# Identity products between two scans, and a blocked triangular solve loaded and stored in parts, in a hybrid DeltaNet and windowed attention layer

## The chip, the cores and the metric

The kernel runs on one core of a Trainium2 chip. The metric is device time in microseconds (us) of one execution of the whole layer. The core's engines are PE (TensorE, matrix products), DVE (VectorE), ACT (ScalarE), POOL (GpSimd) and SP (SyncE, which here issues all DMAs). Each takes its own queue of instructions in order and waits on semaphores of the others.

## The reference

One layer of a bidirectional encoder on x of 2048 x 1024: RMSNorm, one input projection, two groups of heads side by side, an output projection and the residual. Cut to what matters here:

```python
h = rms_norm(x, norm_w)
dn_q, dn_k, dn_v, dn_z, dn_beta, dn_decay, sw_q, sw_k, sw_v, sw_z = split(h @ w_in)
dn = gated_deltanet_bidir(...)           # 4 heads of 128, forward and backward
sw = windowed_gqa_with_sinks(...)        # 8 query heads of 64, |i-j| <= 128
dn = rms_norm(dn, dn_out_norm_w) * silu(dn_z)
sw = sw * silu(sw_z)
x = x + concat([dn, sw]) @ w_out

# gated DeltaNet, one head, one direction, chunk by chunk:
m = tril(k_beta @ k.T, -1) * decay                   # inside a chunk
t_inv = inverse(eye + m)                             # unit lower triangular
u = t_inv @ (v * beta); w = t_inv @ (k_beta * exp(g))
a_intra = incl_tril(q @ k.T) * decay
def step(state, ...):                                # over the chunks, in order
    v_new = u - w @ state
    o = (q * exp(g)) @ state + a_intra @ v_new
    state = state * exp(g_last) + k_dec.T @ v_new
```

So each of the 4 heads needs, for both directions, the inverse of one triangular matrix per chunk, and then a recurrence over the chunks that can't be done in parallel.

## The kernel before, in words

A first phase computes the norm, the projection (products of 512 columns in three parts of a high and a low half), the attention, and the convolutions and gates of the DeltaNet; q, k, v and the gates go to DRAM. What follows is the DeltaNet, with 16 chunks of 128 rows, head by head (h = 0 to 3), in three functions and a fourth that closes a head:

- `pre_front(h)` goes over four groups of four chunks, in the order 1, 2, 0, 3 (`FRONT`). A group loads kq, vt and the decay rows (dc, exponentials on ACT at L669 for all heads but the first), transposes k and q on PE (tr, L641; ks and jk are what ACT makes of them), forms the products gh (L661), scales them on DVE into `ma` (L670, eight operations a group), and stores the rows of ma in DRAM (`m_d`, L675). Then come the transposes of v (trv, L678) and vs (ACT, L682).
- `pre_back(h)` inverts. It loads the 32 x 32 diagonal blocks of all 128 strips (16 chunks x 4 x 2 directions, one strip to a partition) from m_d into `L0` and `L` (two DMAs, L697 and L698), reorders half of them, and runs a forward substitution of 31 steps on DVE, each a product tm (L705) and a subtraction X (L709). This is called the solve. The inverses X go to DRAM (`x_d`, L710) and come back in another layout, per step hi = 0 to 3 a block `xc` for each direction (L718): group hi forward, group 3 - hi backward. DVE transposes it (xt, L719), POOL spreads it into iv (L724 to L728), and five passes of four products on PE (pi, L733) with copies on ACT between them (b and the copies at L742 to L757) build the inverse of the whole 128 x 128 chunk.
- `scan(h)` is the recurrence: 16 steps, each for both directions, forward from chunk 0 and backward from chunk 15. A step loads kqc (L771), and does the products pk, py and po on PE (L773 to L800), r and the state S on DVE, yk and y on ACT, and the sums oacc.
- `post` normalises the output of finished groups (jko, oacc, the transposes tro on PE, zt on DVE) and stores them in `mix_dn` (L843).

The scan of head h needs the inverse for its first chunks at once: forward group 0 and backward group 3, which is hi = 0. Products of the attention half of the output projection (`out_sw`: pcs at L558 to L560, the sums xrs at L561, stored as part) stand in the program between pre_front(0) and pre_back(0). The DeltaNet half of the output projection comes last.

```python
    H = pre_front(0)
    ...                                   # out_sw
    pre_back(0, H)
    for h in range(3):
        scan(h, H)
        H = pre_front(h + 1)
        pre_back(h + 1, H)
    ...
    scan(3, H)
```

This is not the order in which the engines run. A planner (`set_order`) takes all instructions with their dependences and a table of costs, schedules them as a list in several rounds, and writes each engine's queue in the order that it found. So the front and the solve of head h + 1 run beside the scan of head h, and an edit anywhere moves instructions on all five engines.

Buffers are tiles of pools with a number of copies; a tile of the same tag waits for the readers of the copy that it takes over. The PSUM tile `pk` has one copy.

Of the kernel before, what the change touches and what calls it, by code (L numbers as in the profile page):

```python
# [7 lines left out]
F32 = mybir.dt.float32  # L8
# [7 lines left out]
P = 128  # L16
# [3 lines left out]
NCH = 16  # L20
# [496 lines left out]
def phase_b(ctx, tc, t, ident, consts, hp, mix_dn, mix_sw, kq_d, v_d, zdn_d, zsw_d, dp, out):  # L517
    nc = tc.nc
    V, A, G, T = nc.vector, nc.scalar, nc.gpsimd, nc.tensor
    dma = nc.sync.dma_start  # L520

    def pool(name, bufs=1, stack=ctx, **kw):
        return stack.enter_context(tc.tile_pool(name=name, bufs=bufs, reuse_waits="tile", **kw))
# [58 lines left out]
    qp = pool("qp", stack=pre_stack)  # L582
    ps_s = pool("ps_s", space=PSUM)
# [12 lines left out]
    def ma_tile(h, p):  # L596
        tag = f"ma{FREED[p] if h > 1 else p}"
        return hd[h % 2].tile([P, 4, 4, P], F32, tag=tag, name=f"ma{h}_{p}", bufs=1)

    def kv_tile(kind, h, n, name):  # L600
        p, slot = ((0, n), (1, n), (2, n) if n < 2 else (0, n - 2), (0, 2 + n) if n < 2 else (1, n - 2))[h]
        return (hd[p] if p < 2 else qp).tile([P, 4, P], F32, tag=f"{kind}{slot}", name=name, bufs=1)

    def pre_front(h):
        H = {}
        ssk = hp.tile([P, NCH], F32, tag="ssk", name=f"ssk{h}", bufs=1)
        nk = hp.tile([P, NCH], F32, tag="nk", name=f"nk{h}", bufs=1)
        bp = hp.tile([P, 2, NCH], F32, tag="bp", name=f"bp{h}")
        ssq = H["ssq"] = hp.tile([P, NCH], F32, tag="ssq", name=f"ssq{h}", bufs=3)
        ck = H["ck"] = hp.tile([P, 2, NCH], F32, tag="ck", name=f"ck{h}", bufs=3)  # L610
        ks = H["ks"] = {}
        vs = H["vs"] = {}
        mp = {}
        ma = H["ma"] = {}
        m_d = dp.tile([2, NCH, 4 * (32 * P + 32)], F32, tag="m_d", name=f"m_d{h}", bufs=2)
        x_d = dp.tile([2, NCH, P, 32], F32, tag="x_d", name=f"x_d{h}", bufs=2)
        for n, c4 in enumerate(FRONT):
            s4 = slice(4 * c4, 4 * c4 + 4)
            cs = slice(c4 * 512, (c4 + 1) * 512)
            kq = q1.tile([P, 2, 512], F32, tag="kq", name=f"kq{h}_{c4}", bufs=2)  # L620
            dma(kq, kq_d[h][:, :, cs])
            vt = q1.tile([P, 512], F32, tag="vt", name=f"vt{h}_{c4}", bufs=2)
            dma(vt, v_d[h][:, cs])
            gms = []
            for d in range(2):
                gm = q1.tile([P, 4, P], F32, tag="gm", name=f"dc{h}_{c4}_{d}", bufs=4)
                if h < NDEC:
                    dma(gm.rearrange("p c i -> p (c i)"), dec_d[h, d][c4])
                else:
                    src = gr_d[d].rearrange("(c h) i -> c h i", h=4)[s4, h]  # L630
                    dma(gm, src.partition_broadcast(P))
                    G.tensor_tensor(gm, gm, dmask[:, d : d + 1].to_broadcast([P, 4, P]), ALU.add)
                gms.append(gm)
                p = 3 - c4 if d else c4
                if p not in mp:
                    mp[p] = ma_tile(h, p)
                ma[d, c4] = mp[p][:, :, 1 - d :: 2]
            for j, ss in ((0, ssk), (1, ssq)):
                tr = ps_t.tile([P, 4, P], F32, tag="tr", name=f"tr{h}_{c4}_{j}")
                for c in range(4):  # L640
                    T.transpose(tr[:, c], kq[:, j, c * P : (c + 1) * P], ident)  # L641
                if j == 0:
                    ks[c4] = kv_tile("ks", h, n, f"ks{h}_{c4}")
                    A.activation(ks[c4], tr, AF.Copy)
                for c in range(4):
                    cc = 4 * c4 + c
                    src = ks[c4] if j == 0 else tr
                    jk = q1.tile([P, P], F32, tag="jk", name=f"jk{h}_{c4}_{j}_{c}", bufs=3)
                    A.activation(jk, src[:, c], AF.Square, accum_out=ss[:, cc : cc + 1])
            V.tensor_scalar(ssk[:, s4], ssk[:, s4], EPS, None, ALU.add)  # L650
            G.tensor_tensor(nk[:, s4], ssk[:, s4], pw[:, 0, :4], ALU.pow)
            V.reciprocal(ssk[:, s4], ssk[:, s4])
            V.tensor_tensor(
                bp[:, :, s4], beta[:, s4, h :: 4].rearrange("p c d -> p d c"),
                ssk[:, s4].unsqueeze(1).to_broadcast([P, 2, 4]), ALU.mult,
            )
            for c2 in range(2):
                gh = ps_g.tile([P, 2, 2, P], F32, tag="gh", name=f"gh{h}_{c4}_{c2}")
                for k in range(2):
                    c = 2 * c2 + k  # L660
                    T.matmul(  # L661
                        gh[:, k], kq[:, 0, c * P : (c + 1) * P], kq[:, :, c * P : (c + 1) * P], start=True, stop=True
                    )
                for k in range(2):
                    c = 2 * c2 + k
                    cc = 4 * c4 + c
                    for d in range(2):
                        if h >= NDEC:
                            A.activation(gms[d][:, c], gms[d][:, c], AF.Exp, bias=ngc[:, d, cc, h : h + 1])  # L669
                        V.scalar_tensor_tensor(  # L670
                            ma[d, c4][:, c], gh[:, k], bp[:, d, cc : cc + 1],
                            gms[d][:, c : c + 1].to_broadcast([P, 2, P]), ALU.mult, ALU.mult,
                        )
            for d in range(2):
                dma(m_d[d, s4, : P * P].rearrange("u (i j) -> i u j", j=P), ma[d, c4][:, :, 0])  # L675
            tr = ps_t.tile([P, 4, P], F32, tag="tr", name=f"trv{h}_{c4}")
            for c in range(4):
                T.transpose(tr[:, c], vt[:, c * P : (c + 1) * P], ident)  # L678
            vs[c4] = kv_tile("vs", h, n, f"vs{h}_{c4}")
            for c in range(4):  # L680
                cc = 4 * c4 + c
                A.activation(vs[c4][:, c], tr[:, c], AF.Copy, scale=nk[:, cc : cc + 1])  # L682
        for d in range(2):
            V.tensor_tensor(ck[:, d], bp[:, d], ekd[:, d, :, h], ALU.mult)

        H["solve"] = m_d, x_d, mp
        return H

    def pre_back(h, H):
        ma = H["ma"]  # L690
        m_d, x_d, mp = H["solve"]
        L0 = qp.tile([64, 32, 32], F32, tag="L0", name=f"L0{h}")
        L = qp.tile([P, 32, 32], F32, tag="L", name=f"L{h}")
        X = qp.tile([P, 32, 32], F32, tag="X", name=f"X{h}")
        lv = [m_d[d].rearrange("u (p y) -> (u p) y", p=4)[:, : 32 * P] for d in range(2)]
        lv = [a.rearrange("q (r x) -> q r x", x=P)[:, :, :32] for a in lv]
        dma(L0, lv[0])  # L697
        dma(L[64:128], lv[1])  # L698
        dma(X, t["eye32"].partition_broadcast(P))
        V.tensor_copy(L[0:64], L0.rearrange("p r c -> p c r"))  # L700
        for c in range(31):
            n = 31 - c
            tm = qp.tile([P, 256], F32, tag="tm", name=f"tm{h}_{c}")
            tv = tm[:, : n * (c + 1)].rearrange("p (r k) -> p r k", k=c + 1)
            XE.tensor_tensor(  # L705
                tv, L[:, c + 1 :, c : c + 1].to_broadcast([P, n, c + 1]),
                X[:, c : c + 1, 0 : c + 1].to_broadcast([P, n, c + 1]), ALU.mult,
            )
            XE.tensor_tensor(X[:, c + 1 :, 0 : c + 1], X[:, c + 1 :, 0 : c + 1], tv, ALU.subtract)  # L709
        dma(x_d.rearrange("d u (p r) c -> (d u p) (r c)", p=4), X.rearrange("p r c -> p (r c)"))  # L710
        for hi in range(4):
            e1, p2, e2, e3 = (z[hi % len(z)] for z in zts)
            m = mp[hi]
# [1 line left out]
            for d, c4 in ((0, hi), (1, 3 - hi)):  # L715
                xc = qp.tile([P, 4, 32], F32, tag="xc", name=f"xc{h}_{d}_{c4}", bufs=4)
                xt = qp.tile([P, 4, 32], F32, tag="xt", name=f"xt{h}_{d}_{c4}", bufs=4)
                dma(xc, x_d[d, 4 * c4 : 4 * c4 + 4].rearrange("u i c -> i u c"))  # L718
                V.transpose(xt.rearrange("p u c -> p (u c)"), xc.rearrange("p u c -> p (u c)"))  # L719
                x0[d], x1[d] = (xc, xt) if d == 0 else (xt, xc)  # L720
            g = qp.tile([P, 4, P], F32, tag="g", name=f"g{h}_{hi}", bufs=2)
# [111 lines left out]
    def post_rows(h, oa, so, c4):  # L833
# [8 lines left out]
        V.scalar_tensor_tensor(zt, tr.rearrange("p c i -> p (c i)"), dnw, zt, ALU.mult, ALU.mult)  # L842
        dma(mix_dn[h, :, c4 * 512 : (c4 + 1) * 512], zt)  # L843

    H = pre_front(0)
    with tc.using_default_side("right"):
        with ExitStack() as sw:
# [4 lines left out]
            )  # L852
        hd[1] = pool("hd1")
    pre_back(0, H)
    for h in range(3):
        scan(h, H)
        H = pre_front(h + 1)
        pre_back(h + 1, H)
    pre_stack.close()
    op = pool("op", 4)  # L860
    ps_c = pool("ps_c", 4, space=PSUM)
# [362 lines left out]
```

## Time and profile before

| | |
|---|---|
| median of three runs | 1340.53 us (1336.61 to 1341.32) |
| the profiled execution | 1339.74 us, span 1338.0 us |
| mean granted TensorE clock | 0.979 |
| busy: PE, DVE, ACT, POOL | 1258.0, 885.6, 711.3, 484.4 us |
| DMA | 150 GB/s in the mean |

The profile is of one execution. Its views are: the page (busy time, the span in 40 slices with the granted clock of PE in tenths, the costliest groups); busy times of the engines in chosen stretches of time, with the granted clock (1.00 is full speed); the timeline of one engine, where a row gives start, length, line, operation, output and inputs, and in brackets the idle time before it with what ended it; the chain of waits, which follows the end of a stretch back through what released each step; and the time from issue to landing of the DMAs. PE products of fp32 show as two records each.

### The profile page before, as it was taken

The numbers are of one execution on the slowest core, as the hardware profiler recorded it, in microseconds if no ns is written. First come the engines' busy times: TensorE is split into PE (matmuls) and PEld (weight loads), VectorE is DVE, ScalarE is ACT, GpSimd is POOL, SyncE is SP. The second block draws the span as 40 slices with busy tenths as digits, with TensorE's granted clock in tenths as the row PEclk, the third lists the DMA queues.
The fourth block names the chain that finished last, engine by engine and source line by source line (L and its number), as shares of the span: only waits on it lengthen the run. The fifth ranks groups of instructions, "written<-read, shape, count | busy, mean of one in ns | idle before, by whom it ended". The sixth has DMA issues, their size and how long they took to land.

```text
span 1338.0 us, 22553 instructions
## 1 busy us (share of the span) xinstructions
PE 1258.0 (94%) x7162; PEld 1072.9 (80%) x7162; DVE 885.6 (66%) x2250; ACT 711.3 (53%) x2105; POOL 484.4 (36%) x868
## 2 busy tenths in 40 slices
PE   5999999999999999999999899998979879898998
PEld 4998878788998888888888687778868769788776
DVE  4423387773632399999987899666885877846433
ACT  5422264332433467666667877229868766466310
POOL 1223032100021235755786755228238155170000
PEclk8999999999999999999999999999979989989999
DMA  7442345244443533222334757968567274333776
GB/s 235 135 140 78 104 161 171 73 135 135 148 121 114 163 102 109 72 93 83 96 120 130 249 185 226 291 209 217 144 184 207 84 212 104 94 104 106 233 241 209
DMA packets 219686, 201.16 MB, mean 150 GB/s; under 512 B 48304, under 2 KB 170800, under 8 KB 219568
## 3 DMA queue, kind: packets, MB, share of 16 engines
q1 hardware_dynamic: 219568, 199.73, 48.8%
q8 instruction: 57, 0.93, 0.3%
q14 instruction: 61, 0.50, 0.1%
HBM read 134.59 MB, written 65.08 MB: 149 GB/s over the span
## 4 chain that ended last, share of the span: by engine, by line
PE 72%; DVE 9%; DMA 5%; ACT 5%; POOL 5%; issue 3%; SPq 0%; DVEq 0%; POOLq 0%; ACTq 0%
PE pf_c L186 6%; PE pf_c L187 6%; PE pf_c L188 5%; PE pf_z L186 4%; PE pf_z L187 4%; PE pf_z L188 4%; PE pi L733 4%; PE pt L360 2%; PE pq_q L197 2%; PE pq_q L199 2%; PE pq_q L198 2%; PE pcd L559 2%; PE pcd L560 2%; PE pcd L558 2%; PE pcs L558 2%
## 5 line engine op out<-in xcount | busy, mean ns | idle before, releaser
L237 DVE SCALAR_TENSOR_TENSOR acc<-pf_c,cw,acc 128x512 f32<-128x512 f32 (+1 forms) x192 | 140.0, 745 | 22.7 <-ACT acc L233 20.9
L186 PE MATMUL pf_c<-xhi,wh_c 128*128 128x512 f32 x384 | 149.3, 401 | 1.9 <-DVE acc L237 1.1
L187 PE MATMUL pf_c<-xlo,wh_c 128*128 128x512 f32 x384 | 150.4, 401 | 0.0
L188 PE MATMUL pf_c<-xhi,wl_c 128*128 128x512 f32 x384 | 148.4, 400 | 0.0
L186 PE MATMUL pf_z<-xhi,wh_z 128*128 128x512 f32 x256 | 91.6, 400 | 0.1
L355 POOL TENSOR_SCALAR pr<-pr,st 128x384 f32<-128x384 f32 (+1 forms) x128 | 83.5, 670 | 22.5 <-DVE st L353 19.0
L187 PE MATMUL pf_z<-xlo,wh_z 128*128 128x512 f32 x256 | 91.0, 397 | 0.0
L346 ACT ACTIVATE pr<-pr,st 128x384 f32<-128x384 f32 (+1 forms) x128 | 76.2, 598 | 27.3 <-DVE st L345 26.7
L188 PE MATMUL pf_z<-xhi,wl_z 128*128 128x512 f32 x256 | 90.3, 396 | 0.0
L186 PEld LDWEIGHTS pf_c<-xhi,wh_c 128*128 128x128 f32 x384 | 72.3, 189 | 17.5 <-DVE acc L237 1.9
L188 PEld LDWEIGHTS pf_c<-xhi,wl_c 128*128 128x128 f32 x384 | 72.0, 188 | 14.6
L187 PEld LDWEIGHTS pf_c<-xlo,wh_c 128*128 128x128 f32 x384 | 72.3, 188 | 13.9
L341 DVE CUSTOM_DVE_ANT_0 pr<-s,mask,sink 128x384 f32<-128x384 f32 (+1 forms) x128 | 72.6, 594 | 6.0 <-PE pt L360 2.5
L360 PE MATMUL pt<-ident,pr 128*128 128x128 f32 x368 | 72.8, 276 | 3.3 <-ACT q L323 1.4
L364 ACT ACTIVATE ph<-pt 128x512 fp32r<-128x512 f32 x92 | 53.4, 594 | 40.2 <-PE pt L360 37.3
L365 DVE TENSOR_TENSOR pl<-pt,ph 128x512 fp32r<-128x512 f32 x92 | 62.5, 684 | 9.1 <-ACT ph L364 7.9
L670 DVE SCALAR_TENSOR_TENSOR ma<-gh,bp,dc 128x256 f32<-128x256 f32 x128 | 56.1, 476 | 17.7 <-PE gh L661 10.0
L787 ACT ACTIVATE yk<-py,ck 128x128 f32<-128x128 f32 x120 | 44.0, 367 | 40.4 <-PE py L782 39.1
L360 PEld LDWEIGHTS pt<-ident,pr 128*128 128x128 f32 x368 | 48.6, 141 | 19.2 <-POOL pr L355 4.8
L178 DVE TENSOR_TENSOR wl_c<-ws_c,wh_c 128x512 fp32r<-128x512 f32 x48 | 36.6, 765 | 37.0 <-ACT wh_c L177 24.7
L197 PE MATMUL pq_q<-wh_q,xhi 128*128 128x256 f32 x256 | 58.5, 284 | 0.8 <-ACT sgq L256 0.8
L561 DVE TENSOR_TENSOR xrd<-xrd,pcd 128x512 f32<-128x512 f32 x32 | 20.9, 684 | 55.5 <-PE pcd L560 55.5
(250 smaller groups left out, 3769.9 us busy)
## 6 DMA issues: line engine op xcount, KB each, us to landing
kqc<-kq_d SPq DMA_DIRECT2D x120, 128.0 KB, 2.5
ws_c<-wt SPq DMA_DIRECT2D x48, 256.0 KB, 3.5
xr<-x SPq DMA_DIRECT2D x16, 512.0 KB, 6.0
ws_z<-wt SPq DMA_DIRECT2D x32, 256.0 KB, 3.4
kq<-kq_d SPq DMA_DIRECT2D x16, 512.0 KB, 4.9
xrs<-x SPq DMA_DIRECT2D x32, 256.0 KB, 3.4
part<-xrs SPq DMA_DIRECT2D x32, 256.0 KB, 3.4
m_d<-ma SPq DMA_DIRECT2D x32, 256.0 KB, 4.9
```

Of the source, the lines that this page charges most:

```text
L186: T.matmul(ps, hi[:, k, cs], xhi[b][:, k], start=(k == 0), stop=False)
L187: T.matmul(ps, hi[:, k, cs], xlo[b][:, k], start=False, stop=False)
L188: T.matmul(ps, lo[:, k, cs], xhi[b][:, k], start=False, stop=(k == KC - 1))
L197: T.matmul(ps[:, :n], xh, hi[:, k, :n], start=(k == 0), stop=False)
L237: V.scalar_tensor_tensor(av, ps[:, lo:], cw[:, i, k : k + 1], av, ALU.mult, ALU.add)
L341: V.tensor_tensor_reduce(pr[j][:, :n], ps[:, :n], mask[:, lo * P : hi * P], 1.0, sink[:, hh : hh + 1], ALU.add, ALU.max, accum_out=mx[:, j ...
L346: A.activation(pr[j][:, :n], pr[j][:, :n], AF.Exp, bias=nm[:, j : j + 1], accum_out=den[:, j : j + 1])
L355: G.tensor_scalar(pr[j][:, :n], pr[j][:, :n], den[:, j : j + 1], 1.0, ALU.mult, ALU.mult)
L360: T.transpose(pt[:, j], pr[j][:, (kb - lo) * P : (kb - lo + 1) * P], ident)
L365: V.tensor_tensor(pl, ptf, ph.bitcast(F32), ALU.subtract)
L558: T.matmul(ps, mh[:, k], wh[:, k, ns], start=(k == 0), stop=False)
L670: V.scalar_tensor_tensor(ma[d, c4][:, c], gh[:, k], bp[:, d, cc : cc + 1], gms[d][:, c : c + 1].to_broadcast([P, 2, P]), ALU.mult, ALU.mult,)
```

## The change

Three edits, and what the planner makes of them.

First, a function `warm(h)`, called behind pre_back(h + 1) for h = 0, 1, 2. It issues 32, 32 and 20 products of the 128 x 128 identity with itself into a tile of the tag pk, and nothing reads the result. By the tile's tag they stand between the last pk of scan h and the first of scan h + 1.

Second, the DRAM tile m_d is split by group. Each group's diagonal blocks are loaded in pre_front, right behind its stores, with 16 partitions a DMA: eight DMAs a head instead of two. L0 and L, of which there is one copy, are now allocated in pre_front, so the loads of the next head wait for the last tm of the solve before.

Third, x_d is split into three tiles with three stores: forward group 0 (16 partitions), backward group 3 (16 partitions), and the other 96. The loads of hi = 0 read the first two.

```diff
-        m_d = dp.tile([2, NCH, 4 * (32 * P + 32)], F32, tag="m_d", name=f"m_d{h}", bufs=2)
-        x_d = dp.tile([2, NCH, P, 32], F32, tag="x_d", name=f"x_d{h}", bufs=2)
+        L0 = qp.tile([64, 32, 32], F32, tag="L0", name=f"L0{h}")
+        L = qp.tile([P, 32, 32], F32, tag="L", name=f"L{h}")
+        x_d = [dp.tile([4 * n, P, 32], F32, tag=f"x_d{j}", name=f"x_d{h}_{j}", bufs=2) for j, n in enumerate((1, 1, 6))]
...
+            m_d = dp.tile([2, 4, 4 * (32 * P + 32)], F32, tag=f"m_d{n}", name=f"m_d{h}_{c4}", bufs=2)
             for d in range(2):
-                dma(m_d[d, s4, : P * P].rearrange("u (i j) -> i u j", j=P), ma[d, c4][:, :, 0])
+                dma(m_d[d, :, : P * P].rearrange("u (i j) -> i u j", j=P), ma[d, c4][:, :, 0])
+            for d in range(2):
+                lv = m_d[d].rearrange("u (p y) -> (u p) y", p=4)[:, : 32 * P]
+                lo = 64 * d + 16 * c4
+                dma((L if d else L0)[lo : lo + 16], lv.rearrange("q (r x) -> q r x", x=P)[:, :, :32])
...
-        dma(L0, lv[0])
-        dma(L[64:128], lv[1])
...
-        dma(x_d.rearrange("d u (p r) c -> (d u p) (r c)", p=4), X.rearrange("p r c -> p (r c)"))
+        for a, lo, hi in zip(x_d, (0, 112, 16), (16, 128, 112)):
+            dma(a.rearrange("u (p r) c -> (u p) (r c)", p=4), X[lo:hi].rearrange("p r c -> p (r c)"))
...
-                dma(xc, x_d[d, 4 * c4 : 4 * c4 + 4].rearrange("u i c -> i u c"))
+                lo = 4 * (3 * d + c4 - 1 + d)
+                dma(xc, (x_d[2][lo : lo + 4] if hi else x_d[d]).rearrange("u i c -> i u c"))
...
+    def warm(h):
+        idle = ps_s.tile([P, P], F32, tag="pk", name=f"warm{h}")
+        for _ in range((32, 32, 20)[h]):
+            T.matmul(idle, ident, ident, start=True, stop=True)
...
         pre_back(h + 1, H)
+        warm(h)
```

PE's queue at the end of scan 0, before the change (py and po are the scan's last step; gh, tr and trv belong to the front of head 2, tro to the output of head 0, pi to the inverses of head 1; lines behind L613 carry a shift of 1 to 8 in the changed kernel):

```order
L661 MATMUL gh_2_0_12136<-kq_2_12094 128x256 x2
L782 MATMUL py_1_15_10558<-r_1_15_10556,ma_3_8726 128x128
...
L800 MATMUL po_1_15_10559<-y_1_15_10562,ma_3_8726 128x128
L661 MATMUL gh_2_1_12147<-kq_2_12094 128x256 x2
L661 MATMUL gh_0_0_12214<-kq_0_12170 128x256 x2
L641 MATMUL tr_3_0_12258<-ident,kq_3_12248 128x128 x4
L661 MATMUL gh_0_1_12225<-kq_0_12170 128x256 x2
L641 MATMUL tr_3_1_12273<-ident,kq_3_12248 128x128 x4
L839 MATMUL tro_0_10591<-ident,oacc_0_9914 128x128 x4
L839 MATMUL tro_3_10604<-ident,oacc_3_9927 128x128
L733 MATMUL pi_1_0_11053<-iv_0_8564,g_0_11039 128x128 x4
```

And after the change, the same place:

```order
L802 MATMUL po_1_15_10572<-y_1_15_10575,ma_3_8735 128x128
L642 MATMUL tr_3_0_12329<-ident,kq_3_12319 128x128 x4
L850 MATMUL warm_11325<-ident 128x128 x5
L662 MATMUL gh_0_1_12293<-kq_0_12238 128x256 x2
L850 MATMUL warm_11325<-ident 128x128 x9
L662 MATMUL gh_3_0_12361<-kq_3_12319 128x256 x2
L850 MATMUL warm_11325<-ident 128x128 x9
L642 MATMUL tr_3_1_12344<-ident,kq_3_12319 128x128 x4
L850 MATMUL warm_11325<-ident 128x128 x2
L684 MATMUL trv_3_12388<-ident,vt_3_12321 128x128 x2
L841 MATMUL tro_0_10604<-ident,oacc_0_9927 128x128
L735 MATMUL pi_1_0_11079<-iv_0_8564,g_0_11065 128x128 x4
```

Of the 32 identity products 25 stand here between the front's products, seven more among the last py and po ahead of it; one gh (gh_3_0) came in ahead of the first pi and most of tro went behind it. Behind scans 1 and 2 they stand likewise: in the second in runs of 2, 4, 10, 15 and 1, in the third of 2 and 11 ahead of the first pi pass and 4, 2 and 1 behind it.

DVE's queue at the end of head 0's solve, before (X and tm are the solve, xrs the sums of the attention half):

```order
L709 TENSOR_TENSOR X_9536<-X_9536,tm_28_9625 128x3x29
L561 TENSOR_TENSOR xrs_0_9456<-xrs_0_9456,pcs_0_9458 128x512
L705 TENSOR_TENSOR tm_29_9628<-L_9535,X_9536 128x60
L709 TENSOR_TENSOR X_9536<-X_9536,tm_29_9628 128x2x30
L705 TENSOR_TENSOR tm_30_9631<-L_9535,X_9536 128x31
L709 TENSOR_TENSOR X_9536<-X_9536,tm_30_9631 128x31
L561 TENSOR_TENSOR xrs_1_9473<-xrs_1_9473,pcs_1_9475 128x512
L561 TENSOR_TENSOR xrs_0_9496<-xrs_0_9496,pcs_0_9498 128x512
```

And after:

```order
L561 TENSOR_TENSOR xrs_0_9511<-xrs_0_9511,pcs_0_9513 128x512
L709 TENSOR_TENSOR X_9549<-X_9549,tm_25_9627 128x6x26
L705 TENSOR_TENSOR tm_26_9630<-L_8582,X_9549 128x135
L561 TENSOR_TENSOR xrs_1_9528<-xrs_1_9528,pcs_1_9530 128x512
L709 TENSOR_TENSOR X_9549<-X_9549,tm_26_9630 128x5x27
L705 TENSOR_TENSOR tm_27_9633<-L_8582,X_9549 128x112
...
L705 TENSOR_TENSOR tm_30_9642<-L_8582,X_9549 128x31
```

Before, three sums of the attention half followed the solve's tm_28 or later, the last of them behind its end; after, the last sum of all (xrs_1_9528) stands ahead of the X of tm_26. On PE, the first pi pass of head 0 stands behind the last product of the attention half in both kernels; between the two, PE now has 16 transposes and two gh products of the front of head 1.

SP's queue at the end of head 2's solve, before:

```order
L771 DMA kqc_0_3_12801<-kq_d_89 128x2x128
L771 DMA kqc_1_3_12821<-kq_d_89 128x2x128
L631 DMA dc_3_0_13648<-gr_d 128x4x128
L631 DMA dc_3_1_13651<-gr_d 128x4x128
L710 DMA x_d_12015<-X_12328 128x1024
L675 DMA m_d_13410<-ma_2_13423 128x4x128
L771 DMA kqc_0_4_12841<-kq_d_89 128x2x128
L771 DMA kqc_1_4_12862<-kq_d_89 128x2x128
L718 DMA xc_0_0_12427<-x_d_12015 128x4x32
```

And after:

```order
L681 DMA L_13516<-m_d_1_13586 16x32x32
L773 DMA kqc_0_3_12906<-kq_d_89 128x2x128
L773 DMA kqc_1_3_12926<-kq_d_89 128x2x128
L632 DMA dc_3_0_13765<-gr_d 128x4x128
L677 DMA m_d_2_13665<-ma_2_13531 128x4x128
L711 DMA x_d_0_12075<-X_12400 16x1024
L711 DMA x_d_1_12076<-X_12400 16x1024
L632 DMA dc_3_1_13768<-gr_d 128x4x128
L711 DMA x_d_2_12077<-X_12400 96x1024
...
L677 DMA m_d_2_13665<-ma_1_13527 128x4x128
L720 DMA xc_0_0_12499<-x_d_0_12075 128x4x32
```

A load of L for head 3, which waits for the last tm of head 2's solve, now stands in front of these rows, the store of m_d has moved ahead of the store of X, and a second store of m_d stands ahead of the first load of xc. SP issues 33 more instructions in all.

More of the change, by code (lines that the diff above doesn't have):

```diff
@@ L684, in pre_front @@
             V.tensor_tensor(ck[:, d], bp[:, d], ekd[:, d, :, h], ALU.mult)
-        H["solve"] = m_d, x_d, mp
+        H["solve"] = L0, L, x_d, mp
         return H
@@ L690, in pre_back @@
         ma = H["ma"]
-        m_d, x_d, mp = H["solve"]
-        L0 = qp.tile([64, 32, 32], F32, tag="L0", name=f"L0{h}")
-        L = qp.tile([P, 32, 32], F32, tag="L", name=f"L{h}")
+        L0, L, x_d, mp = H["solve"]
         X = qp.tile([P, 32, 32], F32, tag="X", name=f"X{h}")
-        lv = [m_d[d].rearrange("u (p y) -> (u p) y", p=4)[:, : 32 * P] for d in range(2)]
-        lv = [a.rearrange("q (r x) -> q r x", x=P)[:, :, :32] for a in lv]
-        dma(L0, lv[0])
-        dma(L[64:128], lv[1])
         dma(X, t["eye32"].partition_broadcast(P))
```

## The prediction

> **What bounds the kernel now.** I read the page first, then the busy time of the engines by stage, then the chain of waits in the four gaps ahead of the scans.
>
> ```profile
> span 1338.0 us, 22553 instructions
> PE 1258.0 (94%) x7162; PEld 1072.9 (80%) x7162; DVE 885.6 (66%) x2250; ACT 711.3 (53%) x2105; POOL 484.4 (36%) x868
> PEclk8999999999999999999999999999979989989999
> ```
>
> PE is busy for 94% of the span, so only its gaps and its lost clock can go. The granted clock has one low slice, the thirtieth, and a few at 8; they lie where one head's scan hands over to the next. The stages (columns: PE, PEld, DVE, ACT, POOL busy; granted clock; DMA share; GB/s):
>
> ```profile
> 893.80:908.80 15.00, 11.56 (x76) 10.28 (x76) 6.47 (x21) 10.37 (x49) 12.20 (x38) 0.89 0.51 137
> 908.80:949.40 40.60, 38.04 (x288) 34.94 (x287) 27.09 (x84) 37.70 (x158) 28.88 (x57) 1.00 0.88 226
> 949.40:986.80 37.40, 34.11 (x230) 29.84 (x228) 35.63 (x133) 25.34 (x115) 4.07 (x3) 0.91 0.39 115
> 986.80:1010.40 23.60, 17.31 (x99) 14.75 (x99) 14.24 (x45) 18.47 (x77) 16.77 (x37) 0.78 0.96 256
> 1010.40:1030.20 19.80, 19.75 (x162) 18.87 (x161) 13.05 (x41) 15.52 (x59) 17.21 (x46) 1.00 0.87 227
> 1030.20:1082.80 52.60, 43.52 (x305) 38.08 (x304) 45.01 (x157) 38.32 (x163) 15.57 (x20) 0.97 0.40 118
> 1082.80:1106.10 23.30, 17.86 (x99) 15.02 (x99) 12.69 (x41) 15.02 (x66) 15.27 (x40) 0.85 0.70 194
> 1106.10:1117.60 11.50, 11.21 (x91) 10.60 (x90) 6.29 (x20) 7.63 (x27) 9.18 (x27) 1.00 0.64 140
> 1160.00:1182.00 22.00, 18.44 (x105) 15.89 (x103) 9.14 (x33) 10.39 (x44) 10.76 (x34) 0.80 0.45 125
> 1182.00:1338.00 156.00, 145.80 (x830) 124.11 (x829) 71.87 (x175) 56.90 (x186) 19.41 (x52) 0.99 0.58 185
> 991.30:1001.50 10.20, 7.23 (x25) 5.90 (x26) 6.11 (x18) 8.70 (x42) 6.36 (x14) 0.50 1.00 255
> 1172.30:1179.00 6.70, 5.92 (x28) 5.66 (x28) 0.51 (x2) 3.56 (x18) 5.91 (x18) 0.50 0.28 73
> ```
>
> The rows from 893.8, 986.8, 1082.8 and 1160.0 are what I call T0 to T3: from the end of a head's solve to its first scan step. In T1 to T3 PE is idle for 6.3, 5.4 and 3.6 us (15.3 in all) at clocks of 0.78, 0.85 and 0.80; inside them are stretches at 0.50. The stage from 908.8 is scan 0 up to the solve of head 1, with PE (38.0 of 40.6) and ACT (37.7) both nearly full; from 949.4 and 1030.2, beside a solve, DVE leads (35.6 of 37.4, 45.0 of 52.6). The last 156 us are ordered as before but for the queues' first rows; I cost them at nothing, as they already run at 0.99.
>
> **The change part by part.** The terms are set against the profiled execution, 1339.74 us (a span of 1338.0 and 1.7 around it). It lies 0.8 below the median of 1340.53, so 0.8 is added at the end.
>
> *T0, where nothing is warmed.* The planner now puts the last sum of the attention half ahead of nine of the solve's last operations on DVE. That sum needs the last pcs product. DVE's order in time, and the chain:
>
> ```profile
> 885.18 0.30 DVE L709 TENSOR_TENSOR X<-X,tm 128x135 f32<-128x135 f32 x1
> ...
> 886.58 0.69 DVE L561 TENSOR_TENSOR xrs<-xrs,pcs 128x512 f32<-128x512 f32 x1
> ...
> 887.91 0.19 DVE L709 TENSOR_TENSOR X<-X,tm 128x31 f32<-128x31 f32 x1
> ```
> ```profile
> 893.86 0.69 DVE xrs L561
> 894.55 0.23 DVE xt L719
> ...
> 896.16 2.09 PE pi L733 x8
> ...
> 899.26 1.80 ACT jk L649 x13
> ...
> 902.76 1.15 ACT vs L682 x4
> ```
>
> Before, the last X was done at 888.10, the last sum started at 893.86, and the sum stood in front of the transposes xt. From the X at 885.18 to the end is 2.92 us, less one sum of about 0.6 that stood in between: 2.3. Now the sum ends at 894.55 and those 2.3 us follow it: 896.9, or 8.8 later. Against this, the stores of X for the first groups are an eighth as large, and the transposes no longer wait for the sum. What the transfers take, issue to landing (this and the next fence), and SP's issues, one at T0 and two at T1:
>
> ```profile
> x_d<-X SPq DMA_DIRECT2D x1, 512.0 KB, 2.7
> xc<-x_d SPq DMA_DIRECT2D x5, 64.0 KB, 2.4
> ```
> ```profile
> x_d<-X SPq DMA_DIRECT2D x1, 512.0 KB, 5.9
> ```
> ```profile
> 890.80 0.92 SPq L718 DMA_DIRECT2D xc<-x_d  x2
> ...
> 986.79 0.33 SPq L710 DMA_DIRECT2D x_d<-X  x1
> ...
> 992.73 0.37 SPq L718 DMA_DIRECT2D xc<-x_d  x1
> ```
>
> At T0 the whole X landed in 2.7 us. For 64 KB I take 2.2, a little under the 2.4 of the loads of that size: -0.5. The loads issued at 890.8 landed 2.4 later, about 893.2, and the transposes came at 894.55: -1.4. T0: 8.8 - 0.5 - 1.4 = **+6.9**. Its lower bound is +2 (the sum is overtaken by a faster PE in front of it), its upper +12 (PE's 11.6 busy us at half clock instead of 0.89 cost 9 more, half of it on the path).
>
> *Scan 0.* In that longer wait PE now does the front of one more group of head 1: its transposes, gh products and what ACT makes of them. For ACT a group is 0.60 for ks, 2.2 for the 16 records of jk (1.80 / 13 each, above), 1.15 for vs (above) and 2.34 for dc, 6.3 in all; for PE, 12 transposes and 4 products, with pieces of the chain at T1 as prices (these at half clock):
>
> ```profile
> L644 ACT ACTIVATE ks<-tr 128x512 f32<-128x512 f32 x16 | 9.6, 598 | 16.4 <-PE pcs L560 10.3 <-PE tr L641 6.0
> ```
> ```profile
> 992.74 2.34 ACT dc L669 x8
> ...
> 996.34 1.09 PE tr L641 x4
> 997.43 1.72 PE gh L661 x4
> ```
>
> At full clock that is 3 x 0.55 + 2 x 0.86 = 3.4 us of PE. Both engines are nearly full from 908.8, so scan 0 loses between 3.4 and 6.3. By the order of DVE's queue the solve of head 1 also begins at step 6 instead of 8, which lets DVE use its idle third there. I take **-5.5**, with bounds of -10 and 0: nothing, if the eight ma operations that now fall into the solve's own window lengthen it by as much.
>
> *Scans 1 and 2.* With the diagonal blocks of a group loaded as soon as its ma is stored, the solves start earlier against the scan's steps: by the order of DVE's queue about 1.4 steps in scan 1 and 0.75 in scan 2; they end at the same step. The steps before them are 19.8 / 5 = 4.0 and 11.5 / 3 = 3.8 us, with DVE idle for 34% (13.05 of 19.8) and 45% (6.29 of 11.5). The idle that is filled: 1.4 x 4.0 x 0.34 = **-1.9** and 0.75 x 3.8 x 0.45 = **-1.3**; bounds for each -4 and +1, the latter if SP's 32 more issues, at 0.33 apiece, delay the kqc loads.
>
> *T1.* From the store of X to the first load of xc passed 5.94 us. A store of 64 KB lies between 2.4 (the loads) and 5.9 (this store in the same traffic, DMA share 0.96); I take 4.0: -1.9. The 32 identity products stand in PE's gaps from the last scan step on. If they hold the clock, the four transposes and two gh products of the chain above (2.8 us) cost half: -1.4. And the first pi pass, four products, costs 0.22 apiece instead of 0.43:
>
> ```profile
> 955.68 0.89 PE pi L733 x8
> ```
> ```profile
> 1171.68 1.56 PE L733 MATMUL pi<-iv,g 128*128 128x128 f32 x8 [1.34 <-POOL iv L724]
> 1174.01 2.05 PE L733 MATMUL pi<-b,iv 128*128 128x128 f32 x8 [0.78 <-ACT b L742]
> 1175.85 1.91 PE L733 MATMUL pi<-iv,b 128*128 128x128 f32 x8
> 1177.56 0.85 PE L733 MATMUL pi<-iv,g 128*128 128x128 f32 x3
> ```
>
> Eight records are four products: 0.89 / 4 = 0.22 at full clock, and (1177.56 - 1175.85) / 4 = 0.43 at half. That would save 0.8; I take half, as the gaps after that pass hold no identity products: -0.4. T1: **-3.7**, bounds -8 and 0.
>
> *T2.* The row's clock of 0.85 on 17.9 busy us costs 2.7; half of it on the path gives -1.3. Here 25 products stand in runs of 10 and 15, 2.2 and 3.3 us, where PE's two long waits were 1.43 and 1.56:
>
> ```profile
> 1092.42 1.13 PE L661 MATMUL gh<-kq 128*128 128x256 f32 x4 [1.43 <-DVE ma L670]
> 1095.11 1.50 PE L839 MATMUL tro<-ident,oacc 128*128 128x128 f32 x5 [1.56 <-ACT oacc L836]
> ```
>
> That is 2.5 too much, of which I put 1.0 on the path, as the second run ends ahead of the pi pass, which waits for its loads anyway. On SP the first store of X now stands behind a load of L, which waits for the solve's last tm, and behind kqc, dc and m_d; and the load of xc behind another m_d store: +0.3. T2: **0**, bounds -3 and +4.
>
> *T3.* From 1172.3 PE is busy 5.92 us at 0.50: 2.96 less at full clock. Eleven products (2.4 us) stand ahead of the first pi pass in a wait of 1.34, +1.1; four (0.88) ahead of the second in a wait of 0.78, +0.1; three stores where one was, +0.3. T3: **-1.5**, bounds -5 and +1.
>
> Sum: 6.9 - 5.5 - 1.9 - 1.3 - 3.7 + 0 - 1.5 = -7.0; 1339.74 - 7.0 = 1332.7, and with 0.8 **1333.5 us**.
>
> **The rivals.**
>
> *The identity products don't buy the clock and stand in the way (slower).* All 84 at 0.43 are 36.3 us, and the idle in T1 to T3 is 15.3. So up to 21.0 us don't fit; half of that on the path is 10.5, and the clock's share of my terms (1.4 + 0.4 + 1.3 + 3.0, about 6) is lost: 1333.5 + 16.5 = **1350**. It decides as soon as the clock in T1 to T3 still shows stretches at 0.50 while the products run. For it speaks the row from 991.3: PE was busy for 71% there and got 0.50 throughout, so being mostly busy isn't enough. Against it, the row from 1010.4: 99.7% busy had 1.00 throughout, right behind T1. [...]
>
> *The split store buys nothing.* The three parts share the queues, so the first lands when the whole would have: 1.9 at T1, 0.5 at T0 and about 0.5 at T2 and T3 are lost, 2.9 in all: **1336.4**. Against: a load of 64 KB took 2.4 us where the store of 512 KB took 5.9 or 2.7. [...]
>
> *The scans are no shorter for the earlier solves.* Each window ends at the same step as before, so the 8.7 us of the three scan terms may be work that only moves: **1342.2**, no change. For it: PE's 43.5 of 52.6 from 1030.2 leaves little to win. Against: the fuller ACT stage of scan 0.
>
> **How the numbers follow.** About 0.5%, 6.7 us, is what a measurement of this kernel can tell from no change: under 1333.8 is faster, over 1347.2 slower. The forecast gets 0.55, with its own range of 1321 to 1341; it lies at the edge, so I share it as 0.34 faster and 0.21 no change. The split store 0.07 and the scans 0.12, both as no change but for 0.02 that T0's upper bound makes slower. The identity products in the way 0.26: slower but for 0.02, which is a mild form. That makes 0.34 + 0.02 (a split store that gains all the same) faster, 0.38 no change, 0.26 slower. The range of 1319 to 1351 leaves out about half of the slower rival and a twentieth of the forecast below.
>
> **What would show it.** Right: no stretch at 0.50 longer than 2 us in T1 to T3; the last X of head 0 behind the last sum, about 9 us later against the attention half; the first xc load at T1 some 4 us behind the store of X; from the first scan step to the end of scan 0's solve some 5 us less. Wrong: pi passes that begin at once behind an identity product with their operands long there; T0 longer than I think, with PE at half clock; or a solve window that grows by as much as it starts earlier.

## The result and the profile after

The changed kernel takes 1346.59 us (median of five runs, 1345.25 to 1348.67) against 1341.05 us before (1336.61 to 1341.76): a ratio of 1.0052, with a 95% interval of 1.0034 to 1.0070. It is half a per cent slower, where the prediction had said 0.5% faster, 1333.5 us.

The page of the changed kernel, its profiled execution being 1346.25 us:

```profile
span 1344.3 us, 22922 instructions
...
PE 1270.2 (94%) x7330; PEld 1086.1 (81%) x7330; DVE 890.5 (66%) x2250; ACT 710.7 (53%) x2105; POOL 485.3 (36%) x868
...
PEclk9999999999999999999999899999989999999999
```

The low slice of the granted clock is gone, as was meant (7 tenths before, the lowest now 8), PE is busy for 12 us more, and the span is 6.3 us longer. The stages, cut at the same events as before (the last X of a head's solve, the first py of a scan; columns as before):

```profile
903.60:923.40 19.80, 15.72 (x92) 13.06 (x92) 10.49 (x33) 13.80 (x61) 14.79 (x38) 0.83 0.81 207
923.40:999.30 75.90, 69.48 (x506) 63.77 (x507) 63.34 (x214) 60.11 (x252) 35.01 (x65) 0.96 0.61 164
999.30:1023.10 23.80, 20.39 (x149) 19.09 (x148) 11.51 (x37) 15.71 (x68) 14.60 (x37) 0.93 0.93 258
1023.10:1095.20 72.10, 62.80 (x471) 56.91 (x470) 57.32 (x191) 53.34 (x222) 32.51 (x62) 0.98 0.48 131
1095.20:1115.80 20.60, 19.70 (x157) 18.46 (x155) 13.39 (x42) 14.02 (x62) 13.20 (x33) 1.00 0.90 236
1115.80:1167.70 51.90, 48.19 (x382) 44.90 (x380) 45.03 (x154) 35.01 (x129) 23.81 (x57) 1.00 0.31 84
1167.70:1189.40 21.70, 20.03 (x146) 18.09 (x146) 9.38 (x30) 11.66 (x47) 10.90 (x34) 0.93 0.53 136
1189.40:1344.30 154.90, 145.29 (x828) 123.73 (x826) 71.13 (x174) 56.13 (x184) 19.39 (x52) 1.00 0.58 185
```

Set against the kernel before, in us:

| from | to | before | after | change | predicted |
|---|---|---|---|---|---|
| start | first py of scan 0 | 908.8 | 923.4 | +14.6 | +6.9 |
| first py | last X of head 1 (scan 0) | 78.0 | 75.9 | -2.1 | -5.5 |
| T1 | | 23.5 | 23.8 | +0.3 | -3.7 |
| scan 1 | | 72.1 | 72.1 | 0.0 | -1.9 |
| T2 | | 23.7 | 20.6 | -3.1 | 0 |
| scan 2 | | 53.9 | 51.9 | -2.0 | -1.3 |
| T3 | | 21.9 | 21.7 | -0.2 | -1.5 |
| first py of scan 3 | end | 156.1 | 154.9 | -1.2 | 0 |

All of the loss lies ahead of scan 0, where there is no identity product; behind it 8.3 us come back. So the question is what delays head 0. First DVE before, then DVE after: the last ma of head 0's front, the first tm of its solve, the last sum of the attention half and the last X.

```profile
833.95 1.27 DVE L670 SCALAR_TENSOR_TENSOR ma<-gh,bp,dc 128x256 f32<-128x256 f32 x3
...
855.11 0.20 DVE L705 TENSOR_TENSOR tm<-L,X 128x31 f32<-128x31 f32 x1
```
```profile
844.54 1.26 DVE L671 SCALAR_TENSOR_TENSOR ma<-gh,bp,dc 128x256 f32<-128x256 f32 x3
...
871.97 0.21 DVE L705 TENSOR_TENSOR tm<-L,X 128x31 f32<-128x31 f32 x1
...
900.61 0.68 DVE L561 TENSOR_TENSOR xrs<-xrs,pcs 128x512 f32<-128x512 f32 x1
...
903.45 0.19 DVE L709 TENSOR_TENSOR X<-X,tm 128x31 f32<-128x31 f32 x1
```

The front ends 10.6 us later (845.8 against 835.2), the solve begins 16.9 later and ends 15.5 later. From the start of the last sum to the last X it is 3.0 us, as predicted (0.7 and 2.3); but the sum starts at 900.61 and not at 893.86. Its row has no idle time in brackets, so DVE came to it without a wait; before, DVE waited 0.44 us for this sum's product. Six us between front and solve came on top of the late front. They show in SP's timeline, before and after:

```profile
838.87 0.67 SPq L675 DMA_DIRECT2D m_d<-ma  x1
847.03 0.61 SPq L697 DMA_DIRECT2D L<-m_d  x1
847.68 3.11 SPq L698 DMA_DIRECT2D L<-m_d  x1
```
```profile
846.71 0.38 SPq L677 DMA_DIRECT2D m_d<-ma  x1
...
855.60 0.48 SPq L677 DMA_DIRECT2D m_d<-ma  x1
...
866.02 1.13 SPq L681 DMA_DIRECT2D L<-m_d  x2
```

Before, the last store of head 0's diagonal rows went out 3.7 us behind the last ma; after, 9.8, and the last loads of L 10.4 us behind that store (before, 8.2).

### The profile page after: what moved, and what is told of

It is laid out like the page before. It is cut to its first block, busy times and chain, and to the rows that moved or that the text cites. A ratio compares the mean times of both kernels' runs of the same rounds, so it can differ in the third digit from the quotient of the medians.

```text
span 1344.3 us, 22922 instructions
## 1 busy us (share of the span) xinstructions
PE 1270.2 (94%) x7330; PEld 1086.1 (81%) x7330; DVE 890.5 (66%) x2250; ACT 710.7 (53%) x2105; POOL 485.3 (36%) x868
## 4 chain that ended last, share of the span: by engine, by line
PE 71%; DVE 10%; DMA 7%; ACT 5%; POOL 3%; issue 3%; SPq 1%; DVEq 0%; ACTq 0%; POOLq 0%
PE pf_c L186 6%; PE pf_c L187 6%; PE pf_c L188 6%; PE pf_z L186 4%; PE pf_z L187 4%; PE pf_z L188 4%; PE pi L735 3%; PE pt L360 3%; PE pq_q L197 2%; PE pq_q L198 2%; PE pq_q L199 2%; PE pcs L558 2%; PE pcs L559 2%; PE pcs L560 2%; PE py L784 2%
## 5 line engine op out<-in xcount | busy, mean ns | idle before, releaser
L188 PE MATMUL pf_z<-xhi,wl_z 128*128 128x512 f32 x256 | 93.2, 398 | 0.0
L188 PEld LDWEIGHTS pf_c<-xhi,wl_c 128*128 128x128 f32 x384 | 72.1, 188 | 14.7
L789 ACT ACTIVATE yk<-py,ck 128x128 f32<-128x128 f32 x120 | 43.9, 366 | 41.6 <-PE py L784 40.6
L177 ACT ACTIVATE wh_c<-ws_c 128x512 fp32r<-128x512 f32 x48 | 29.6, 627 | 56.1 <-PE pf_z L187 24.1
```

The costliest lines, as they stand in the source:

```text
L188: T.matmul(ps, lo[:, k, cs], xhi[b][:, k], start=False, stop=(k == KC - 1))
```

## The experiments

Ratios are of a kernel's time to that of the kernel before on the same chip, with 95% intervals; "planned anew" means that the planner ordered all queues for that kernel.

**Parts, planned anew.** The edits are left out or taken alone; e1:

```diff
         pre_back(h + 1, H)
-        warm(h)
```

> The changed kernel without its 84 identity products, newly planned (group loads and split store stay). Theory A (the group loads of the diagonal blocks cost: they bring head 0's solve to its end 15.5 us late, and the products win some 3 us behind scan 1): solve 0 still ends near 903 us instead of 888, the gap behind scan 1 is back near 23.5 us, and the kernel is slower than the changed one: about 1350 us. Theory B (the products stand in the way and cost what was lost): without them the kernel is at 1341 us or below.

> The kernel before with the group loads alone (no products, one store of X). Theory A: solve 0 ends about 15 us later than in the kernel before, and the time is 1348 to 1352 us. Theory B: no loss, 1341 us. If the loss came from the split store, 1341 us too, and e1 would be slow.

> The kernel before with the products and the split store, without the group loads. Theory A: solve 0 ends near 888 us as before, the gap behind scan 1 falls to some 20.5 us, time about 1337 us. Theory B: 1345 us or more.

> The kernel before with the identity products alone. Theory A: about 1338 us; if the split store is worth its 1.9 us in the gap behind scan 0, this is 1 to 2 us above e3, if it is worth nothing, the same as e3. Theory B: 1345 us or more.

| kernel | median us | ratio | first tm, last X of head 0 |
|---|---|---|---|
| e1: group loads, split store | 1352.02 | 1.0093 (1.0070 to 1.0116) | 875.2, 905.3 |
| e2: group loads | 1350.73 | 1.0068 (1.0045 to 1.0091) | 872.0, 903.0 |
| e3: products, split store | 1341.64 | 1.0013 (0.9999 to 1.0027) | 854.9, 887.9 |
| e4: products | 1345.24 | 1.0030 (1.0015 to 1.0045) | 859.9, 894.7 |

With the group loads head 0's solve ends 15 to 17 us later than before, and the kernel loses 0.7 to 0.9%. Without them it loses 0.1% (e3, not told apart from nothing) and 0.3% (e4, whose solve ends 6.6 us late although it has no group loads). That is in the main theory A and against theory B. But A had also said that the products then win some 3 us, and e3 and e4 are no faster than the kernel before. In e3 T1 and T2 took 19.8 and 19.7 us (23.5 and 23.7 before), and scan 0 up to the last X of head 1 took 90.7 (78.0): the gaps gave 7.7 us, and scan 0 took 12.7 more in the new order. So I formed theory C, that planning anew costs in itself, and a way to test an edit without it.

**Edits with the queues kept.** The planner is shown the kernel before, and what is added is put into the finished queues. For e5 these are 46 products ahead of PE's longest waits of the profile before:

```diff
+PLACE = {"gh2_2_1": 6, "gh2_0_0": 8, "tr2_3_0": 6, "gh3_0_1": 5, "gh3_3_0": 6, "tro1_0": 7, "pi0_3_0": 5, "pi1_3_0": 3}
...
+            if o[0].startswith("warm"):
+                added.append((i, eng))
...
+            for at in [p for p in left if name.startswith(p + "_")]:
+                for _ in range(left.pop(at)):
+                    line.append(added.pop(0)[0])
+            line.append(insts[k][0])
```

In e6 the three stores of X stand where the one stood; e7 has both. e8 keeps the program and changes one number of the planner:

```diff
-LAG = {"PE": 205, "DVE": 140, "Activation": 160, "Pool": 120, "SP": 2400}
+LAG = {"PE": 206, "DVE": 140, "Activation": 160, "Pool": 120, "SP": 2400}
```

> The kernel before with every engine's queue in the order it had, and 46 identity products put into PE's longest waits of the profile before (20, 18 and 8 behind scans 0, 1 and 2), of which the planner knows nothing. Theory C (each edit makes the planner order everything anew, and that costs some 10 us up to the end of head 1's solve; the products themselves gain behind the scans): the last X of head 1 ends near 987 us as before, no long stretch at half clock in the gaps, time 1334 to 1338 us. Theory B (the products cost): 1341 us or more with the gaps as long as before. Theory D (the clock in the gaps is not on the path): the clock is full and the time 1340 to 1342 us.

> The kernel before with the split store alone, every queue in the order it had (SP issues three stores where one was). If the first part lands earlier and its load goes out earlier: the gap behind scan 0 is 1.9 us shorter, the others 0.5 to 1.5: 1337 to 1339 us. If three parts through the same queues land as one: 1341 us, or 1 us more for the two issues more a head.

> Products and split store, every queue in the order of the kernel before. Theory C: the sum of what e5 and e6 gain, 1332 to 1336 us, the fastest so far. Theory D: as e6.

> The kernel before with one number of the planner's table changed, PE's lag of 205 ns to 206: the same instructions, planned anew into other queues. Theory C: slower than the kernel before by some 5 to 12 us, with the last X of head 1 at 992 us or later. If the plan is not what costs (theory A alone, the group loads): 1338 to 1343 us.

| kernel | median us | ratio |
|---|---|---|
| e5: products, queues kept | 1339.64 | 0.9989 (0.9975 to 1.0003) |
| e6: split store, queues kept | 1341.14 | 1.0001 (0.9988 to 1.0013) |
| e7: both, queues kept | 1340.98 | 0.9994 (0.9977 to 1.0011) |
| e8: lag 206, planned anew | 1338.62 | 0.9979 (0.9964 to 0.9994) |

e8 takes theory C down, in which planning anew costs in itself: another plan can be a little faster. And e5 shows what the products are worth alone: about 1.5 us, not told apart from nothing. Its gaps T1, T2 and T3, and rows of PE inside them:

```profile
988.40:1013.60 25.20, 20.08 (x138) 17.69 (x137) 14.40 (x44) 19.23 (x78) 17.80 (x40) 0.95 0.93 259
1086.10:1107.70 21.60, 18.70 (x135) 16.62 (x135) 13.40 (x43) 14.92 (x66) 14.31 (x37) 1.00 0.76 212
1161.20:1181.60 20.40, 17.75 (x118) 15.34 (x118) 9.25 (x33) 10.61 (x45) 9.39 (x29) 0.92 0.47 133
```
```profile
998.06 0.63 PE L641 MATMUL tr<-ident,kq 128*128 128x128 f32 x4 [0.92 <-DMA kq<-kq_d]
...
1002.12 1.16 PE L733 MATMUL pi<-iv,g 128*128 128x128 f32 x8 [1.55 <-POOL iv L724]
...
1172.91 1.16 PE L733 MATMUL pi<-iv,g 128*128 128x128 f32 x8 [0.23 <-POOL iv L724]
...
1179.10 0.33 PE L839 MATMUL tro<-ident,oacc 128*128 128x128 f32 x1 [1.29 <-ACT oacc L836]
```

The clock rose from 0.78, 0.85 and 0.80 to 0.95, 1.00 and 0.92, and the first pi pass at T3 takes 1.16 us instead of 1.56. But T2 and T3 are only 2.1 and 1.5 us shorter, and T1 is 1.7 longer. PE works faster and then waits: for iv of POOL, for kq of the DMA queues, for oacc of ACT. This is theory D, for the larger part: the clock was raised, and little of it was on the path.

For the split store, e6 shows the DMAs at T1 and SP's issues:

```profile
x_d<-X SPq DMA_DIRECT2D x1, 384.0 KB, 5.2
x_d<-X SPq DMA_DIRECT2D x2, 64.0 KB, 4.9
```
```profile
989.99 1.26 SPq L711 DMA_DIRECT2D x_d<-X  x3
...
995.06 0.38 SPq L720 DMA_DIRECT2D xc<-x_d  x1
```

A store an eighth as large landed 4.9 us after its issue, beside 5.2 for the rest. The load of xc goes out 5.1 us behind the store and not 5.9, and nothing of that is left in the time: T1 is 23.5 us as before. In the changed kernel the head start at T1 was larger:

```profile
x_d<-X SPq DMA_DIRECT2D x1, 384.0 KB, 5.7
x_d<-X SPq DMA_DIRECT2D x2, 64.0 KB, 3.7
```

**What of the group loads costs.** e9 puts the eight loads where the two stood, in the queues of the kernel before. e10 is the opposite: the program of the kernel before, in the order planned for e2, made by planning e2's program first and using its queues. e11 is the changed kernel, but head 0 has one m_d and two loads:

```diff
...
-            for d in range(2):
+            for d in range(2 if h else 0):
                 lv = m_d[d].rearrange("u (p y) -> (u p) y", p=4)[:, : 32 * P]
...
+        if not h:
+            lv = [m_all[d].rearrange("u (p y) -> (u p) y", p=4)[:, : 32 * P] for d in range(2)]
+            lv = [v.rearrange("q (r x) -> q r x", x=P)[:, :, :32] for v in lv]
+            dma(L0, lv[0])
+            dma(L[64:128], lv[1])
```

e12 is the changed kernel in its own order, with the 84 products taken out of the finished PE queue.

> The kernel before with its queues kept and the eight group loads put where its two loads of a head stood, so that SP issues six more a head at that place. Theory E (the loads themselves are cheap, and the loss comes from where the planner then puts head 0's front): some 1 to 3 us for six issues of 0.4 us ahead of each solve, 1341 to 1345 us. Theory F (SP, which issues in order, is what the loads cost): 1347 us or more.

> The opposite of e9: the kernel before, two loads a head, with every queue in the order that the planner made for the group loads (e2); the two loads stand where the last of the eight stood. Theory E: as slow as e2, 1348 to 1352 us, with the last ma of head 0 near 846 us as there. Theory F: 1343 us or less.

> The changed kernel with head 0's blocks loaded in two DMAs as before, the group loads for heads 1 to 3 alone; products and split store stay; planned anew. Theory A, narrowed to head 0: head 0's solve ends near 888 us again and the time is 1335 to 1341 us. If the group loads of the later heads cost as well: 1345 us or more.

> The changed kernel with every queue in its order and the 84 identity products taken out. If the products gain in this plan what the changed kernel is ahead of e1 (5.4 us): 1350 to 1353 us, with stretches at half clock in all three gaps. If they only fill time and the clock isn't on the path: 1344 to 1348 us, as the changed kernel. If they are in the way: below 1344 us.

| kernel | median us | ratio |
|---|---|---|
| e9: group loads, queues kept | 1341.57 | 1.0015 (1.0002 to 1.0027) |
| e10: two loads, e2's order | 1352.29 | 1.0089 (1.0066 to 1.0111) |
| e11: changed kernel, head 0 loaded in two | 1335.95 | 0.9976 (0.9960 to 0.9993) |
| e12: changed kernel's order, no products | 1348.52 | 1.0068 (1.0046 to 1.0090) |

The first tm, the last X and the first py of head 0: of e9 the first tm, then of e10, then of e11 (lines are shifted in e10 and e11).

```profile
856.56 0.21 DVE L705 TENSOR_TENSOR tm<-L,X 128x31 f32<-128x31 f32 x1 [0.86 <-DMA L<-m_d]
```
```profile
871.06 0.21 DVE L864 TENSOR_TENSOR tm<-L,X 128x31 f32<-128x31 f32 x1 [0.69 <-DMA L<-m_d]
...
904.40 0.19 DVE L868 TENSOR_TENSOR X<-X,tm 128x31 f32<-128x31 f32 x1
...
929.19 0.42 PE L941 MATMUL py<-vs,ma 128*128 128x128 f32 x1
```
```profile
848.93 0.21 DVE L714 TENSOR_TENSOR tm<-L,X 128x31 f32<-128x31 f32 x1 [0.15 <-DMA L<-m_d]
...
885.69 0.19 DVE L718 TENSOR_TENSOR X<-X,tm 128x31 f32<-128x31 f32 x1
...
907.24 0.39 PE L793 MATMUL py<-vs,ma 128*128 128x128 f32 x2
```

e9 and e10 settle it, as theory E had said: with the eight loads in the old order head 0's solve begins 1.5 us later than before, and the kernel loses 0.15%; with the two old loads in the new order it begins at 871.1 and the kernel loses 0.89%, as much as with the group loads themselves. What costs is the order that the planner finds when the loads are there, not the loads. (e10 has the order of e2 and not that of the changed kernel, but head 0's solve begins at 872.0 in both of these.) In e11 the planner has head 0's loads as before: the solve begins at 848.9, and the kernel is faster than the kernel before by 0.24% and some 10 us faster than the changed one.

e12 came out between its cases. Its gaps have a lower granted clock again, 0.87, 0.77 and 0.85 where it was 0.93, 1.00 and 0.93 with the products:

```profile
1001.10:1026.50 25.40, 14.70 (x91) 12.60 (x89) 12.43 (x37) 15.72 (x68) 14.56 (x38) 0.87 0.90 255
1098.60:1121.10 22.50, 16.61 (x92) 13.73 (x91) 13.51 (x42) 13.96 (x62) 15.13 (x40) 0.77 0.88 225
1172.90:1195.20 22.30, 18.05 (x107) 15.28 (x106) 9.26 (x31) 11.73 (x48) 11.69 (x37) 0.85 0.53 131
```

Without products T1 to T3 sum to 70.2 us, with them to 66.1; but e12's profile is of its slowest run, 1351.87 us. Of these 4 us about 2 appear in the medians (1348.52 against 1346.59), and the two intervals overlap. So the 84 products are worth something between nothing and a few us in this order too. The other part of the 5.4 us between e1 and the changed kernel would again be another plan; that is not shown, as the intervals of e1 and e12 overlap.

## Why the prediction was wrong

- **T0, the step that failed.** The working "Now the sum ends at 894.55 and those 2.3 us follow it" put the delay of the last sum at nothing, without a reason: it took the sum's time from the trace of before, though all queues had been ordered anew. The sum ended at 901.3, 6.7 us later. The 2.3 us behind it held, but the wait forecast ahead of it did not come: PE's last product for it was done at 900.5, and DVE came to the sum at 900.6. Both were late by then, PE with its products and DVE with a solve that had begun 16.9 us late (the solve itself took 31.7 us, before 33.0). So sum and solve would each have kept the last X back without the other. The term came to +14.6 instead of +6.9, beyond my upper bound of +12, which was drawn from the clock alone; that is 7.7 of the 13.3 us between the -7.0 forecast and the +6.3 of the span. PE up to the start of the last sum, before and after:

```profile
0.00:893.90 893.90, 863.18 (x4610) 726.05 (x4610) 606.29 (x1379) 449.01 (x1070) 323.32 (x496) 0.99 0.45 144
0.00:900.60 900.60, 867.90 (x4610) 727.58 (x4610) 606.15 (x1369) 448.05 (x1070) 321.05 (x494) 0.99 0.44 142
```

  With as many records, PE was busy 4.7 us longer and idle 2.0 us longer (32.7 against 30.7). An example of such waits, one row of DVE and one of PE, after:

```profile
870.10 0.69 DVE L561 TENSOR_TENSOR xrs<-xrs,pcs 128x512 f32<-128x512 f32 x1 [3.63 <-DMA xrs<-x]
```
```profile
876.82 0.62 PE L558 MATMUL pcs<-wohs,mhs 128*128 128x512 f32 x1 [2.96 <-DVE xrs L561]
```

  A sum waits 3.6 us for its load, which SP issued among those of kqc and L; the solve begins right behind it, and PE then waits 3.0 us for the next sum, which stands among the solve's first operations.
- **Scan 0** gave 2.1 us instead of 5.5, and **scans 1 and 2** 0.0 and -2.0, for -1.9 and -1.3. The first tm of head 1 and of head 2 after:

```profile
953.34 0.21 DVE L705 TENSOR_TENSOR tm<-L,X 128x31 f32<-128x31 f32 x1
...
1037.95 0.19 DVE L705 TENSOR_TENSOR tm<-L,X 128x31 f32<-128x31 f32 x1
```

  The solves did begin earlier against the first py, by 10.7 us in scan 0 (29.9 behind it instead of 40.6) and by 5.1 in scan 1 (14.8 instead of 19.9). But they also took longer, 45.9 us instead of 37.4 and 57.3 instead of 52.2. That is the sign that the prediction had named, a solve window that grows by as much as it starts earlier: wholly so in scan 1, for the most part in scan 0. The rival that the scans are no shorter was half right: the three gave 4.1 us of 8.7.
- **T1.** The clock came as forecast (0.93 instead of 0.78), the time did not. SP's rows show one reason, with the last X done at 999.27:

```profile
1000.47 0.58 SPq L681 DMA_DIRECT2D L<-m_d  x1
1001.56 1.33 SPq L711 DMA_DIRECT2D x_d<-X  x2
...
1005.62 1.47 SPq L720 DMA_DIRECT2D xc<-x_d  x1
```

  From the store to the first load of xc it is 4.1 us instead of 5.9, as forecast. But the store went out 2.3 us behind the last X, and not at once as before, since in SP's queue a load of kqc and the new load of L now stand ahead of it; the prediction had priced such a delay at T2 (0.3) and put it at nothing here. The load of xc therefore left 6.4 us behind the last X, where it was 6.0. PE's rows: full up to 1010, then waiting.

```profile
1007.03 2.17 PE L850 MATMUL warm<-ident 128*128 128x128 f32 x18
...
1011.87 0.44 PE L684 MATMUL trv<-ident,vt 128*128 128x128 f32 x2 [1.78 <-ACT jk L650]
1013.94 0.48 PE L841 MATMUL tro<-ident,oacc 128*128 128x128 f32 x1 [1.64 <-ACT oacc L838]
1014.21 2.05 PE L735 MATMUL pi<-iv,g 128*128 128x128 f32 x8
```

  The waits named here are for ACT; and the last iv of this pass came from POOL at 1014.1, as its xc had landed only at 1012.8. The clock had fallen again by the first pi pass, to 0.50 from 1014.2 to 1016.3, and the pass took 2.05 us for eight records, where e5's took 1.16. I had priced the chain's PE pieces at full clock and asked too little what is late next.
- **T2** went better (-3.1 instead of 0): the long runs of 10 and 15 products did not hold up the pi pass as I had feared, and the clock was 1.00 throughout. **T3** gave 0.2 of the 1.5.
- **The split store** gave nothing that can be measured in the time (e6), so that rival held in its price, but not in its reason: the small parts did land first, 3.7 us after issue beside 5.7 at T1, and their load left earlier behind the store (4.1 us instead of 5.9).
- **The slower rival** had the sign and the wrong mechanism: the identity products don't stand in the way (e12, and e5). (Its 84 products at 0.43 are 36.1 us and not 36.3, which changes nothing.) With the products between transposes and gh products the clock was 1.00 over all of T2, where it was 0.85 before and, without them, 0.77 in e12.

What stays open: why the planner puts head 0's front later when its loads come by group, and which of the moved instructions cost most; e10 shows that the order suffices, not which rows of it. Why PE was busy 4.7 us longer up to the last sum is open too; a lower granted clock in part of the stretch (0.94 from 872.0 to 900.6, where it was 1.00 from 855.1 to 893.9 before) would be some 1.5 us of it, an estimate from 25.6 busy us there. Whether e11's gain comes from the products, the later heads' loads or once more from its plan is not shown: in its profile, which is of its fastest run, T1 to T3 sum to 59.3 us, 9.8 less than before, and scan 0 up to the last X of head 1 takes 85.4, 7.4 more.

## What to carry to other kernels

Where a planner orders the queues, an edit is two edits: the instructions, and the new order of everything else, which here was worth from -0.2% to +0.9%. Keep the queues and put the edit in, or run the old program in the new order, before anything is said of the edit itself; and spare the place where the new order hurts (here head 0), rather than give the edit up. Here a clock raised from 0.78, 0.85 and 0.80 to 0.95, 1.00 and 0.92 in the three gaps (e5) made the second and third 2.1 and 1.5 us shorter and the first 1.7 longer, as PE then waited for other engines and for loads: look first at what the gap's last waits name.

## What the runs showed of the hardware that was not expected

The first part of a split store had a head start of a varying size: at T1 its 64 KB took 4.9 us in e6, where the other 384 KB, issued with it, took 5.2, and 3.7 beside 5.7 in the changed kernel. And the clock at T1 of the changed kernel did not stay up behind the identity products: from 1006.0 to 1010.0 us PE was busy throughout at 1.00, from 1010.0 to 1014.2 it was busy for 0.8 us, and from 1014.2 to 1016.3, in which the first pi pass took 2.05 us, the granted clock was 0.50.
